# Spreading the start addresses of a block kernel's weight, input and activation buffers modulo 512 bytes

## Chip, cores and metric

The kernel runs on one core of a Trainium2 chip. The metric is device time in microseconds for one execution of the whole kernel; lower is better. All numbers in memory are fp32.

## The reference

With depth 1 the reference is one layer: a gated short convolution, then an expert-choice mixture of experts, over 2048 tokens of width 1024, with 16 experts that take 256 tokens each. Cut to what is computed:

```python
m = silu(c) @ ada_w + ada_b                      # six modulation vectors
hl = modulate(rms_norm(x, norm_g[0]), sh1, sc1)  # 2048 x 1024
gate_b, gate_c, v = split(hl @ w_in, 3)          # weights 1024 x 3072
yl = (gate_b * dwconv(gate_c * v, conv)) @ w_out # weights 1024 x 1024
lat = x + g1 * yl
h2 = modulate(rms_norm(lat, norm_g[1]), sh2, sc2)
aff = softmax(h2 @ router)
g, idx = top_k(aff.T, 256)                       # tokens of each expert
hid = silu(h2[idx] @ w_gate) * (h2[idx] @ w_up)  # per expert, 1024 x 1024 each
out = lat + g2 * scatter_add(idx, (hid @ w_down) * g)
```

## The kernel before

Every large product is made of three products in the type fp32r. Each operand is split into a high part (the value cast to fp32r) and a low part (what is left); high x high, high x low and low x high are added up in PSUM. So a weight slot `ws` holds two halves of 4096 bytes in each partition, and the input tiles hold two halves as well.

**Weights.** All weights pass through one list of pieces of 128 x 1024 numbers. SyncE loads a piece into one of three `raw` buffers (`load_piece`), ScalarE casts it into the first half of a slot (`split_high`, L198), VectorE, in some places GpSimd, subtracts to make the second half (`split_low`, L208). There are eight slots (`n_split`), used in turn.

**Stages.** (1) Input product, `in_mm` (L436, L437, L439): 128 columns of a slot are loaded into the array, and 512 columns of the input tile `hl` are streamed past them; nine matmuls to each of eight contraction steps, 32 such groups. (2) Output product and router, `out_mm` (L641, L642, L644): here a block of `hl` is loaded and 512 columns of a slot are streamed, six matmuls to each contraction step; the router's small products (L708, L709) stand among them. (3) A search for the thresholds of each expert's 256 tokens. (4) The experts: `gate_up` (L1010, L1012, L1014) loads 128 columns of a slot and streams 256 columns of the expert's gathered input `xT`; `down` (L1032 to L1034) loads 128 columns of the activations `hT` and streams 512 columns of a slot. From the third expert on one period is `gate_up` of a half, `down` of half of the expert before, and the same again.

**Order.** Nothing is moved by a scheduler: the program runs as written, and a matmul waits only where its slot, its input or its PSUM bank is not ready. Each matmul has a load of its own, which the array takes while the matmul before it still streams.

**Addresses.** Tiles are placed one behind the other in each partition. In the built program before the change all eight slots start at 384 modulo 512 (they are 8192 bytes apart), all `hl` buffers at 288, and `xs`, both `xT` and all four `hT` at 64. The *distance* of a matmul is here the start of the operand that is being loaded (for the next matmul) minus the start of the one that is streamed, modulo 512. Offsets inside these tiles are multiples of 512, so before the change each product has one distance: 96 in `in_mm`, 416 in `out_mm`, 320 in `gate_up`, 192 in `down`. Where one product follows another, the distance is another for that one matmul: 0 from `down` to `gate_up`, for instance.

The pools are `weights` (`raw` and `ws`), `small`, and `mix` (stages 1 and 2: `hl` and work tiles), whose room is later taken by `moe` (stage 4: `xs`, `xT`, `hT`, `sg`, `ot`). A tile of `moe` waits for the last users of the room that it takes.

Of the kernel before, what the change touches and what calls it, by code (L numbers as in the profile page):

```python
# [7 lines left out]
F32 = mybir.dt.float32  # L8
F32R = mybir.dt.float32r
# [7 lines left out]
P = 128  # L17
# [3 lines left out]
CAP = 256  # L21
KD = D // P
# [18 lines left out]
def block_kernel(ctx: ExitStack, tc, x, c, ada_w, ada_b, norm_g, w_in, conv, w_out, router, wg, wu, wd, out):  # L41
# [3 lines left out]
    wpool = ctx.enter_context(tc.tile_pool(name="weights", bufs=1))  # L45
# [3 lines left out]
    n_raw, n_split = 3, 8  # L49
# [120 lines left out]
    pieces, n_load, n_high, n_done = [], 0, 0, 0  # L170
    ws_of = {}
# [15 lines left out]
    def load_to(i):  # L187
        nonlocal n_load
        while n_load <= min(i, len(pieces) - 1, load_end[0] - 1):
            load_piece(n_load)  # L190
            n_load += 1

    def split_high(i):
        nonlocal n_high
        while n_high <= min(i, len(pieces) - 1):
            load_to(n_high)
            t = wpool.tile([P, 2] + pieces[n_high][3], F32R, name="ws", tag="ws", bufs=n_split)
            nc.scalar.activation(t[:, 0], raws[n_high], AF.Copy)  # L198
            ws_of[n_high] = t
            n_high += 1  # L200

    def split_low(i, eng=None, part=0, n=1):
        nonlocal n_done
        split_high(i)
        t, raw = ws_of[i], raws[i]
        w = pieces[i][3][-1] // n
        s = slice(part * w, (part + 1) * w)
        (eng or nc.vector).tensor_sub(t[:, 1, ..., s], raw[..., s], t[:, 0, ..., s].bitcast(F32))  # L208
        if part == n - 1:
            raws.pop(i)  # L210
            n_done += 1
            load_to(i + n_raw)
# [16 lines left out]
    def split_half(i, g, eng=None):  # L229
        nonlocal n_high, n_done  # L230
        if g == 0:
            ws_of[i] = wpool.tile([P, 2] + pieces[i][3], F32R, name="ws", tag="ws", bufs=n_split)
            n_high += 1
        t, n = ws_of[i], pieces[i][3][0] // 2
        s = slice(g * n, (g + 1) * n)
        nc.scalar.activation(t[:, 0, s], raws[i][:, s], AF.Copy)
        (eng or nc.vector).tensor_sub(t[:, 1, s], raws[i][:, s], t[:, 0, s].bitcast(F32))
        if g:
            raws.pop(i)
            n_done += 1  # L240
            load_to(i + n_raw)
# [106 lines left out]
    with tc.tile_pool(name="mix", bufs=1) as mix:  # L348
# [9 lines left out]

        junk = mix.tile([P, D], BF, name="junk")
        carry = mix.tile([P, KD, 3], F32, name="carry")  # L360
        nc.gpsimd.memset(carry, 0.0)

        hl, xq = {}, {}
# [157 lines left out]
        ada_fix(0, pcol)  # L521
        pair = [new_banks() for _ in range(2)]
        split_half(0, 0)
        split_half(1, 0)
        split_half(2, 0, nc.gpsimd)
        to_hl(0, 0, lambda: ada_cols(1, 0, 4))
        ada_cols(1, 4)
# [411 lines left out]


    moe = ctx.enter_context(tc.tile_pool(name="moe", bufs=1, reuse_waits="tile"))
    out_rows = out.rearrange("b t d -> (b t) d")
    H = QT
    idx_of, gate_of, xT_of, hT_of, ot_of, scat = {}, {}, {}, {}, {}, {}
# [34 lines left out]
    def fetch(e, i, bank=None):  # L979
        g, s = divmod(i, 2)  # L980
        if i == 0:
            xT_of[e] = moe.tile([P, 2, KD, CAP], F32R, name="xT", tag="xT", bufs=2)
        xT, xs = xT_of[e], xs_of[e][s]
        pt = (bank or tp).tile([P, 4, P], F32, name="pt", tag="mm" if bank else "tp")
        for j in range(4):
            nc.tensor.transpose(pt[:, j], xs[:, (4 * g + j) * P:(4 * g + j + 1) * P], identf)  # L986
        d = (slice(None), slice(4 * g, 4 * g + 4), slice(s * P, (s + 1) * P))
        nc.scalar.activation(xT[:, 0][d], pt, AF.Copy)
        nc.vector.tensor_sub(xT[:, 1][d], pt, xT[:, 0][d].bitcast(F32))  # L989

    def gate_up(e, fh, between=lambda k: None):
        xT = xT_of[e]
        if fh == 0:
            hT_of[e] = {}
        ps = [[mm.tile([P, 2, CAP], F32, name="pm", tag="mm") for _ in range(2)] for _ in range(2)]
        for kk in range(KD // 2):
            for j in range(2):
                k = 2 * kk + j
                n = w_moe[0, e, fh, kk] + n_split - 2 + j
                if (e, fh) != (0, 1):  # L1000
                    split_high(n)
                between(k)
                while n_done <= min(n, len(pieces) - 1):
                    split_low(n_done, nc.gpsimd if n_done % 2 and (e, fh) < (1, 1) else None)
                for f in range(4):
                    c0 = slice(f * P, (f + 1) * P)
                    for m in range(2):
                        o = ps[m][f // 2][:, f % 2]
                        w = ws_of[w_moe[m, e, fh, kk]]
                        nc.tensor.matmul(o, w[:, 0, j, c0], xT[:, 0, k], start=(k == 0 and f % 2 == 0), stop=False,  # L1010
                                         skip_group_check=True)
                        nc.tensor.matmul(o, w[:, 0, j, c0], xT[:, 1, k], start=False, stop=False,  # L1012
                                         skip_group_check=True)
                        nc.tensor.matmul(o, w[:, 1, j, c0], xT[:, 0, k], start=False, stop=(k == KD - 1),  # L1014
                                         skip_group_check=True)
        hT = moe.tile([P, 2, 4, CAP], F32R, name="hT", tag="hT", bufs=4)
        hT_of[e][fh] = hT
        for f2 in range(2):
            sg = moe.tile([P, 2, CAP], F32, name="sg", tag="sg", bufs=2)
            nc.scalar.activation(sg, ps[0][f2], AF.Silu)  # L1020
            nc.vector.tensor_mul(sg, sg, ps[1][f2])
            t = slice(2 * f2, 2 * f2 + 2)
            nc.scalar.activation(hT[:, 0, t], sg, AF.Copy)
            nc.vector.tensor_sub(hT[:, 1, t], sg, hT[:, 0, t].bitcast(F32))
# [55 lines left out]
    for i in (0, 2, 1, 3):  # L1080
        fetch(0, i, mm)
    for e in range(E):
        if e == 0:
            gate_up(0, 0, lambda k: (tick(k), pick(1) if k == 7 else None))
            gate_up(0, 1, lambda k: fetch(1, k - 4) if k >= 4 else tick(k) if k > 1 else None)
            continue
        if e == 1:
            gate_up(1, 0, lambda k: tick(k) if k > 1 else None)
            down(0, 0, lambda kk: tick(kk) if kk else None)
            for _ in rounds:  # L1090
                pass
            pick_oh(2)
            gate_up(1, 1, lambda k: pick(2) if k == 2 else None)
        else:
            if e + 1 < E:
                pick_oh(e + 1)
            gate_up(e, 0)
            down(e - 1, 0, (lambda kk: pick(e + 1) if kk == 2 else None) if e + 1 < E else (lambda kk: None))
            gate_up(e, 1)
        down(e - 1, 1, (lambda kk: (fetch(e + 1, kk - 1), fetch(e + 1, kk)) if kk % 2 else None)  # L1100
             if e + 1 < E else (lambda kk: None))
# [24 lines left out]
```

## Time and profile before

| | us |
|---|---|
| median of three runs (lowest, highest) | 1984.61 (1983.23, 1985.26) |
| the profiled execution's own time | 1985.33 |
| its span, from first to last instruction | 1983.5 |
| PE busy | 1901.4 (96%) |
| DVE busy | 1130.6 (57%) |
| ACT busy | 751.2 (38%) |
| POOL busy | 306.9 (15%) |

The profiled execution's time stands 0.7 us above the median. A matmul's busy time in the profile covers its whole passage through the array, and neighbours overlap: a row that says 277 ns for one does not mean that one starts every 277 ns. What a matmul costs is read from the *starts*: the difference of two start times, divided by the number of matmuls between them, here called the pace. [...]

### The profile page before, as it was taken

How to read it: one execution, taken by the hardware profiler on the slowest of the kernel's cores; microseconds unless marked ns; L12 is line 12 of the kernel's file. 1: busy time of each engine (PE TensorE's matmuls, PEld its weight loads, DVE VectorE, ACT ScalarE, POOL GpSimd, SP SyncE). 2: the span in 40 equal slices, each digit the busy share in tenths (PEclk: the TensorE clock that was granted, in tenths of full speed). 3: DMA queues.
4: the chain of work that ended last, by engine and by line, in shares of the span. 5: the costliest groups of instructions: out<-in, count | busy, mean ns of one | idle time of the engine just before them, and what ended most of it. 6: DMA issues, size and time to landing. Idle time of an engine off the chain costs nothing.

```text
span 1983.5 us, 29691 instructions
## 1 busy us (share of the span) xinstructions
PE 1901.4 (96%) x11930; PEld 1669.5 (84%) x11930; DVE 1130.6 (57%) x1656; ACT 751.2 (38%) x1050; POOL 306.9 (15%) x521
## 2 busy tenths in 40 slices
PE   4999999999999999659999999999999999999998
PEld 3787788887788888549999999999999999999996
DVE  7544424344334666776665656656665666566653
ACT  3411126211123333345444544444444444444542
POOL 3310011101011222333211011101110110111001
PEclk8999999999999999869999999999999999999999
DMA  9443241433216443235677676767677766777674
GB/s 283 127 133 127 81 144 53 139 127 123 67 64 213 166 149 132 85 127 165 199 222 211 214 233 200 220 217 235 202 214 233 227 201 214 229 209 218 212 212 116
DMA packets 216573, 344.38 MB, mean 174 GB/s; under 512 B 12092, under 2 KB 94068, under 8 KB 216436
## 3 DMA queue, kind: packets, MB, share of 16 engines
q1 hardware_dynamic: 200468, 284.82, 44.6%
q0 software_dynamic: 15968, 57.68, 11.2%
q8 instruction: 93, 1.52, 0.3%
q14 instruction: 44, 0.36, 0.1%
HBM read 300.51 MB, written 41.94 MB: 173 GB/s over the span
## 4 chain that ended last, share of the span: by engine, by line
PE 92%; DVE 3%; DMA 2%; SPq 1%; issue 1%; ACT 1%; POOL 0%; POOLq 0%; DVEq 0%; ACTq 0%
PE pm L1010 11%; PE pm L1012 11%; PE pm L1014 11%; PE pm L436 9%; PE pm L437 9%; PE pm L439 9%; PE pm L1032 6%; PE pm L1034 6%; PE pm L1033 6%; PE pm L641 3%; PE pm L644 3%; PE pm L642 3%; PE pt L986 1%; SPq L399 1%; DVE hl L312 1%
## 5 line engine op out<-in xcount | busy, mean ns | idle before, releaser
L208 DVE TENSOR_TENSOR ws<-raw,ws 128x1024 fp32r<-128x1024 f32 x415 | 499.0, 1223 | 314.4 <-ACT ws L198 312.5
L198 ACT ACTIVATE ws<-raw 128x1024 fp32r<-128x1024 f32 x437 | 451.0, 1054 | 444.2 <-PE pm L1014 208.0
L1010 PE MATMUL pm<-xT,ws 128*128 128x256 f32 x2048 | 569.6, 278 | 0.0
L1012 PE MATMUL pm<-xT,ws 128*128 128x256 f32 x2048 | 567.7, 277 | 0.1
L1014 PE MATMUL pm<-xT,ws 128*128 128x256 f32 x2048 | 567.4, 277 | 0.0
L1012 PEld LDWEIGHTS pm<-xT,ws 128*128 128x128 f32 x2048 | 386.4, 189 | 1.7 <-DVE xT L989 0.4
L1010 PEld LDWEIGHTS pm<-xT,ws 128*128 128x128 f32 x2048 | 386.2, 189 | 1.2
L1014 PEld LDWEIGHTS pm<-xT,ws 128*128 128x128 f32 x2048 | 386.0, 189 | 0.0
L436 PE MATMUL pm<-hl,ws 128*128 128x512 f32 x768 | 311.2, 405 | 1.0 <-ACT hl L386 1.0
L437 PE MATMUL pm<-hl,ws 128*128 128x512 f32 x768 | 307.0, 400 | 0.0
L439 PE MATMUL pm<-hl,ws 128*128 128x512 f32 x768 | 222.7, 398 | 0.0
L1032 PE MATMUL pm<-ws,hT 128*128 128x512 f32 x512 | 203.8, 398 | 0.0
L1034 PE MATMUL pm<-ws,hT 128*128 128x512 f32 x512 | 201.5, 394 | 0.0
L1033 PE MATMUL pm<-ws,hT 128*128 128x512 f32 x512 | 200.0, 391 | 0.0
L436 PEld LDWEIGHTS pm<-hl,ws 128*128 128x128 f32 x768 | 146.4, 191 | 36.6 <-ACT hl L386 1.4
L437 PEld LDWEIGHTS pm<-hl,ws 128*128 128x128 f32 x768 | 146.4, 191 | 35.1 <-issue 1.0
L439 PEld LDWEIGHTS pm<-hl,ws 128*128 128x128 f32 x768 | 145.8, 190 | 35.8
L1058 POOL DMA_INDIRECT out_dram<-ot,idx x32 | 78.5, 2454 | 591.4 <-DVE ot L1052 587.4
L449 DVE TENSOR_TENSOR u<-cs,pm 128x512 f32<-128x512 f32 x32 | 22.5, 703 | 246.0 <-ACT cs L446 246.0
L446 ACT ACTIVATE cs<-pm 128x512 f32<-128x512 f32 x32 | 19.1, 597 | 346.8 <-issue 272.0
L1034 PEld LDWEIGHTS pm<-ws,hT 128*128 128x128 f32 x512 | 96.2, 188 | 20.7
L1033 PEld LDWEIGHTS pm<-ws,hT 128*128 128x128 f32 x512 | 96.3, 188 | 18.9
(267 smaller groups left out, 2026.8 us busy)
## 6 DMA issues: line engine op xcount, KB each, us to landing
raw<-in_moe_w_gate_dram SPq DMA_DIRECT2D x128, 512.0 KB, 4.4
raw<-in_moe_w_up_dram SPq DMA_DIRECT2D x128, 512.0 KB, 4.3
raw<-in_moe_w_down_dram SPq DMA_DIRECT2D x128, 512.0 KB, 4.6
raw<-in_sc_w_in_dram SPq DMA_DIRECT2D x45, 512.0 KB, 4.6
xt<-in_x_dram SPq DMA_DIRECT2D x32, 512.0 KB, 6.2
aw<-in_ada_w_dram SPq DMA_DIRECT2D x32, 512.0 KB, 6.5
hl<-in_ada_w_dram SPq DMA_DIRECT2D x32, 256.0 KB, 5.4
hl<-vscr SPq DMA_DIRECT2D x16, 512.0 KB, 5.0
```

The lines of the kernel that those rows point to most:

```text
L198: nc.scalar.activation(t[:, 0], raws[n_high], AF.Copy)
L208: (eng or nc.vector).tensor_sub(t[:, 1, ..., s], raw[..., s], t[:, 0, ..., s].bitcast(F32))
L436: nc.tensor.matmul(ps[m], wh, t[:, 0], start=(k == 0), stop=False)
L437: nc.tensor.matmul(ps[m], wl, t[:, 0], start=False, stop=False)
L439: nc.tensor.matmul(ps[m], W(k, m)[0], t[:, 1], start=False, stop=(k == KD - 1))
L1010: nc.tensor.matmul(o, w[:, 0, j, c0], xT[:, 0, k], start=(k == 0 and f % 2 == 0), stop=False, skip_group_check=True)
L1012: nc.tensor.matmul(o, w[:, 0, j, c0], xT[:, 1, k], start=False, stop=False, skip_group_check=True)
L1014: nc.tensor.matmul(o, w[:, 1, j, c0], xT[:, 0, k], start=False, stop=(k == KD - 1), skip_group_check=True)
L1032: nc.tensor.matmul(ps[s], h, w[:, 0, j], start=(k == 0), stop=False)
L1033: nc.tensor.matmul(ps[s], h, w[:, 1, j], start=False, stop=False)
L1034: nc.tensor.matmul(ps[s], l, w[:, 0, j], start=False, stop=(k == KD - 1))
L1058: st = nc.gpsimd.indirect_dma_start(out=out_rows, out_offset=bass.IndirectOffsetOnAxis(ap=idx_of[e][:, s:s + 1], axis=0), in_=ots[s], in_o ...
```

## The change

It moves only the places of tiles. The eight slots get a tag each, and there is a pad of 64 bytes ahead of slots 1 to 7, so that they start at 384, 448, 0, 64, 128, 192, 256 and 320 modulo 512. A pad of 32 bytes in `mix` puts the `hl` buffers at 256. A pad of 64 bytes opens `moe`, one of 64 bytes stands ahead of the second `xT` and one of 128 bytes ahead of each `hT` but the first: `xs` stays at 64, `xT` is at 64 for even experts and at 128 for odd ones, the four `hT` are at 64, 256, 384 and 0.

A distance is then always a multiple of 64. In `in_mm`, `out_mm` and `gate_up` all eight multiples occur equally often, and the distance changes from one slot to the next: in `gate_up` after every third matmul. In `down` it is 192, 256, 448 or 0, seldom 128 or 384.

```diff
--- before.py
+++ after.py
@@ -190,11 +190,17 @@
             load_piece(n_load)
             n_load += 1
 
+    def ws_tile(i):
+
+        if 0 < i < n_split:
+            wpool.tile([P, 16], F32, name=f"wpad{i}")
+        return wpool.tile([P, 2] + pieces[i][3], F32R, name="ws", tag=f"ws{i % n_split}", bufs=1)
+
     def split_high(i):
         nonlocal n_high
         while n_high <= min(i, len(pieces) - 1):
             load_to(n_high)
-            t = wpool.tile([P, 2] + pieces[n_high][3], F32R, name="ws", tag="ws", bufs=n_split)
+            t = ws_tile(n_high)
             nc.scalar.activation(t[:, 0], raws[n_high], AF.Copy)
             ws_of[n_high] = t
             n_high += 1
@@ -229,7 +235,7 @@
     def split_half(i, g, eng=None):
         nonlocal n_high, n_done
         if g == 0:
-            ws_of[i] = wpool.tile([P, 2] + pieces[i][3], F32R, name="ws", tag="ws", bufs=n_split)
+            ws_of[i] = ws_tile(i)
             n_high += 1
         t, n = ws_of[i], pieces[i][3][0] // 2
         s = slice(g * n, (g + 1) * n)
@@ -358,6 +364,7 @@
 
         junk = mix.tile([P, D], BF, name="junk")
         carry = mix.tile([P, KD, 3], F32, name="carry")
+        mix.tile([P, 8], F32, name="mixpad")
         nc.gpsimd.memset(carry, 0.0)
 
         hl, xq = {}, {}
@@ -939,6 +946,7 @@
 
 
     moe = ctx.enter_context(tc.tile_pool(name="moe", bufs=1, reuse_waits="tile"))
+    moe.tile([P, 16], F32, name="moepad")
     out_rows = out.rearrange("b t d -> (b t) d")
     H = QT
     idx_of, gate_of, xT_of, hT_of, ot_of, scat = {}, {}, {}, {}, {}, {}
@@ -979,7 +987,9 @@
     def fetch(e, i, bank=None):
         g, s = divmod(i, 2)
         if i == 0:
-            xT_of[e] = moe.tile([P, 2, KD, CAP], F32R, name="xT", tag="xT", bufs=2)
+            if e == 1:
+                moe.tile([P, 16], F32, name="xpad")
+            xT_of[e] = moe.tile([P, 2, KD, CAP], F32R, name="xT", tag=f"xT{e % 2}", bufs=1)
         xT, xs = xT_of[e], xs_of[e][s]
         pt = (bank or tp).tile([P, 4, P], F32, name="pt", tag="mm" if bank else "tp")
         for j in range(4):
@@ -1013,7 +1023,10 @@
                                          skip_group_check=True)
                         nc.tensor.matmul(o, w[:, 1, j, c0], xT[:, 0, k], start=False, stop=(k == KD - 1),
                                          skip_group_check=True)
-        hT = moe.tile([P, 2, 4, CAP], F32R, name="hT", tag="hT", bufs=4)
+        h_i = (2 * e + fh) % 4
+        if 0 < 2 * e + fh < 4:
+            moe.tile([P, 32], F32, name=f"hpad{h_i}")
+        hT = moe.tile([P, 2, 4, CAP], F32R, name="hT", tag=f"hT{h_i}", bufs=1)
         hT_of[e][fh] = hT
         for f2 in range(2):
             sg = moe.tile([P, 2, CAP], F32, name="sg", tag="sg", bufs=2)
```

No instruction of the computation is added, removed or moved on any engine, and the waits of PE, GpSimd and SyncE are the same. Since `moe` takes other parts of the room of `mix`, some waits for that room stand elsewhere on ScalarE and VectorE. One such place is ScalarE at the second half of the first expert: `sg` is the SwiGLU's product, `hT` its cast, and the queues DMASW1, 3 and 7 are those of stores that GpSimd issued in stages 1 and 2. Before:

```order
L198 ACTIVATE ws<-raw 128x1024 [waits DMAHW4_49,Pool_49]
L1020 ACTIVATE sg<-pm 128x512 [waits PE_49]
L1023 ACTIVATE hT<-sg 128x512 [waits DMASW1_49,DVE_49]
L1020 ACTIVATE sg<-pm 128x512 [waits PE_49]
L1023 ACTIVATE hT<-sg 128x512 [waits DVE_49]
```

After:

```order
L204 ACTIVATE ws<-raw 128x1024 [waits DMAHW4_49,Pool_49]
L1033 ACTIVATE sg<-pm 128x512 [waits PE_49]
L1036 ACTIVATE hT<-sg 128x512 [waits DMASW7_49,DMASW3_49,DVE_49]
L1033 ACTIVATE sg<-pm 128x512 [waits PE_49]
L1036 ACTIVATE hT<-sg 128x512 [waits DVE_49]
```

The order is the same; the first cast of this half waits for other store queues.

## Rows read from the trace of the kernel before

**Rows 1.** The page: busy times, and the chain that ended last by engine.

```profile
PE 1901.4 (96%) x11930; PEld 1669.5 (84%) x11930; DVE 1130.6 (57%) x1656; ACT 751.2 (38%) x1050; POOL 306.9 (15%) x521
PE 92%; DVE 3%; DMA 2%; SPq 1%; issue 1%; ACT 1%; POOL 0%; POOLq 0%; DVEq 0%; ACTq 0%
```

**Rows 2.** Groups by line, engine PE: shapes xcount | busy us, mean ns.

```profile
L1010 PE MATMUL pm<-xT,ws 128*128 128x256 f32 x2048 | 569.6, 278 | 0.0
L436 PE MATMUL pm<-hl,ws 128*128 128x512 f32 x768 | 311.2, 405 | 1.0 <-ACT hl L386 1.0
L1032 PE MATMUL pm<-ws,hT 128*128 128x512 f32 x512 | 203.8, 398 | 0.0
L641 PE MATMUL pm<-ws,hl 128*128 128x512 f32 x256 | 106.2, 415 | 0.0
```

**Rows 3.** Chain in order of time (start us, us, what), input product.

```profile
100.71 0.70 PE pm L439 x3
...
166.07 0.70 PE pm L439 x3
```

**Rows 4.** Timeline of PE (start us, us, what), output product.

```profile
648.62 0.39 PE L641 MATMUL pm<-ws,hl 128*128 128x512 f32 x1
...
651.42 0.39 PE L641 MATMUL pm<-ws,hl 128*128 128x512 f32 x1
```

**Rows 5.** Timeline of PE, `down` and the matmul behind it.

```profile
1304.50 0.39 PE L1033 MATMUL pm<-ws,hT 128*128 128x512 f32 x1
...
1309.54 0.40 PE L1034 MATMUL pm<-ws,hT 128*128 128x512 f32 x1
1309.77 0.28 PE L1010 MATMUL pm<-xT,ws 128*128 128x256 f32 x1
```

**Rows 6.** Timeline of PE, `gate_up`, settled.

```profile
1279.79 0.28 PE L1014 MATMUL pm<-xT,ws 128*128 128x256 f32 x1
...
1283.42 0.28 PE L1012 MATMUL pm<-xT,ws 128*128 128x256 f32 x1
```

**Rows 7.** Timeline of PE, first matmuls of that `gate_up`.

```profile
1276.48 0.28 PE L1010 MATMUL pm<-xT,ws 128*128 128x256 f32 x1
...
1277.18 0.28 PE L1010 MATMUL pm<-xT,ws 128*128 128x256 f32 x1
...
1279.00 0.28 PE L1012 MATMUL pm<-xT,ws 128*128 128x256 f32 x1
```

**Rows 8.** Timeline of PE, `gate_up` of expert 1, second half.

```profile
976.32 0.28 PE L1014 MATMUL pm<-xT,ws 128*128 128x256 f32 x1
...
979.97 0.28 PE L1010 MATMUL pm<-xT,ws 128*128 128x256 f32 x1
```

**Rows 9.** Timeline of PE and its loads (PEld), output product into router.

```profile
643.35 0.19 PEld L642 LDWEIGHTS pm<-ws,hl 128*128 128x128 f32 x1
...
643.82 0.63 PE L644 MATMUL pm<-ws,hl 128*128 128x512 f32 x2
644.05 0.11 PEld L708 LDWEIGHTS plt<-hl,rts 128*32 128x32 f32 x1
644.28 0.22 PE L708 MATMUL plt<-hl,rts 128*32 128x128 f32 x1
```

**Rows 10.** Timeline of PE, input product, early.

```profile
49.16 0.63 PE L436 MATMUL pm<-hl,ws 128*128 128x512 f32 x1
...
50.44 0.63 PE L437 MATMUL pm<-hl,ws 128*128 128x512 f32 x1
```

**Rows 11.** Windows: us, busy (x) of engines, PE clock, DMA share, GB/s.

```profile
50.00:51.00 1.00, 1.00 (x4) 0.79 (x3) 0.97 (x4) 0.88 (x2) 0.04 (x1) 0.50 1.01 401
1130.96:1876.13 745.17, 745.17 (x5630) 698.50 (x5628) 462.21 (x539) 342.08 (x396) 80.49 (x55) 1.00 0.72 218
```

**Rows 12.** Chain in order of time, eight transposes in fp32.

```profile
1883.51 0.87 PE pt L986 x8
```

**Rows 13.** Line L681, GpSimd stores of the second stage.

```profile
L681 POOL DMA_DIRECT2D hscr<-u x15: 620/634/643, 632.5 to 817.6; - x15
DMA to landing us min/median/max: 3.0/3.7/4.6
```

**Rows 14.** Line L1023, the casts into `hT`.

```profile
L1023 ACT ACTIVATE hT<-sg x64: 631/632/634, 904.0 to 1943.4; 128x512 fp32r<-128x512 f32 x64
```

## Prediction, made blind

> **What bounds the kernel.** The page comes first: PE is busy for 96% of the span and holds 92% of the chain that ended last [rows 1]. The change touches no instruction, so it can act only on how fast PE streams, or on an engine that feeds PE. The groups by line give the counts [rows 2]: three lines of 2048 are the 6144 matmuls of `gate_up`, three of 768 the 2304 of `in_mm`, three of 512 the 1536 of `down`, three of 256 the 768 of `out_mm`. Their busy times overlap, so the cost is read as a pace from starts:
>
> - `in_mm`: 65.36 us between two rows of the chain, 31 groups of nine matmuls, so 65.36 / 279 = 234.3 ns [rows 3];
> - `out_mm`: 2.80 us for 12 matmuls, 233.3 ns [rows 4];
> - `down`: 5.04 us for 22 matmuls, 229.1 ns [rows 5];
> - `gate_up`, settled: 3.63 us for 32 matmuls, 113.4 ns [rows 6].
>
> [...] And it differs between products of one shape: `in_mm`, `out_mm` and `down` all stream 512 columns past a loaded block of 128, yet differ by 5 ns. What sets `in_mm` and `out_mm` apart from `down` and `gate_up` is that their distances, 96 and 416, are 32 more than a multiple of 64, while 192 and 320 are multiples of 64.
>
> **The change, part by part.** *Removed and added:* nothing. *Moved waits:* ScalarE's and VectorE's waits for the room of `mix` are for stores; of the last of these, those of `hscr`, the last is issued at 817.6 us and lands within 4.6 us, while the first cast into `hT` starts at 904.0 [rows 13, 14]. Whoever waits for them instead finds them done, some 80 us early: 0 us. *Weights, casts, subtractions, DMAs:* the same sizes and counts, off the path in stage 4 (in the long window DVE is busy for 462 of 745 us, ACT for 342, the DMA share is 0.72 [rows 11]): 0 us, and they have room for a PE that is a few per cent faster.
>
> *`in_mm` and `out_mm`:* their distances become multiples of 64, as those of `down` are now. The trace has no row of these two products at such a distance in a steady run, so I bound it. [...] Worst: the slowest pace that fp32r shows at a multiple of 64 is that of an unsettled `gate_up`, 117.7 ns for 256 columns [rows 8], so 235.4 for 512: 2304 x 1.1 + 768 x 2.1 = 4 us more. I take the row that is nearest in shape, `down` with the same 512 columns and a distance that is a multiple of 64: 234.3 - 229.1 = 5.2 ns for 2304 and 233.3 - 229.1 = 4.2 ns for 768, so 12.0 + 3.2 = 15.2 us.
>
> *`down`:* stays at a multiple of 64, only at several of them. Value taken: 0 us; bounds: 1536 x 13.7 = 21 us less (the floor) and 1536 x 5.2 = 8 us more (the pace of `in_mm`).
>
> *`gate_up`:* the same holds, 0 us taken. [...]
>
> Sum: 1985.3 of the profiled execution - 15.2 = 1970.1 us. The median of the runs stands 0.7 us lower than that execution, which is within what I round: 1970 us.
>
> [...] In the trace, the matmul under which only 32 columns are loaded, for the router, at distance 0, keeps the pace: two matmuls take 643.82 to 644.28, 230 ns each [rows 9], and the one that ends `down`, at distance 0 instead of 192, also takes 230 ns [rows 5]. [...]
>
> **Rivals.**
>
> *1. `gate_up` loses its step (slower).* The same instructions at the same addresses have a second pace: for expert 1 the second half runs at 3.65 us for 31 matmuls, 117.7 ns [rows 8], against 113.4. And each `gate_up` opens at that slower pace: the first six matmuls of one take 0.70 us, 116.7 ns each, before it settles [rows 7]. So loads and streams fall into a rhythm after about six matmuls, if nothing disturbs them. After the change the distance differs every third matmul. If each change of distance starts the settling anew, all 6144 stay at 117.7: 6144 x 4.3 = 26 us more, 2012 us; with the gain in `in_mm` and `out_mm` beside it, 1997. It decides against the change as soon as more than 15.2 / 26 = 58% of these matmuls don't settle. Against it: the jump from distance 192 over 0 to 320, where `down` ends, is repaired within those six matmuls, and a step of 64 may be no disturbance at all.
>
> [...]
>
> *3. Nothing (same).* [...] The rows of the switches speak for it.
>
> **How the numbers follow.** The measurement tells some 0.2%, 4 us, from no change. The forecast, `in_mm` and `out_mm` gain and the rest stays within a few us, has 0.36; rival 2, in whole or half, 0.16; rival 3 0.24; rival 1, enough to outweigh the gain, 0.24. So faster 0.52, same 0.24, slower 0.24. The range goes from 1928 us, just past the half of rival 2 (0.08 lies below), to 2002 us, which holds rival 1 with the gain beside it and most of its single form's partial cases (0.10 lies above). The forecast's own range, with `down` and `gate_up` a little off zero, is 1955 to 1979 us.
>
> **What would show it.** Right: groups of nine `in_mm` matmuls at 2.06 us instead of 2.11, six of `out_mm` at 1.37 to 1.38 instead of 1.40, `down` at 229 ns and settled `gate_up` at 113.4. Rival 1: `gate_up` starts near 117 ns apart beyond its first six matmuls. [...] Rival 3: all four paces as before. Wrong in kind would be a change of DVE or ACT durations, a new wait for a slot, or a stretch of PE at the lower clock.

## The result and the profile after

The change makes the kernel slower: 2003.11 us (four runs, 2002.79 to 2007.04) against 1984.71 before, a ratio of 1.0098 with a 95% interval of 1.0081 to 1.0116. That is 1 us above the forecast range, and 33 us above the forecast.

The page of the changed kernel shows as many matmuls and weight loads as before; PE and its loads (PEld) are busier, the other engines hardly differ [rows 1]:

```profile
span 2001.6 us, 29694 instructions
PE 1921.2 (96%) x11930; PEld 1693.8 (85%) x11930; DVE 1129.5 (56%) x1656; ACT 750.2 (37%) x1050; POOL 308.8 (15%) x521
PE 93%; DVE 4%; issue 1%; DMA 1%; ACT 1%; POOL 1%; SPq 0%; POOLq 0%; DVEq 0%; ACTq 0%
```

In stage 4 PE is busy without a break and at the upper clock, as before (the same stretch as in [rows 11]: window, then PE, PEld, DVE, ACT and POOL busy, clock, DMA share, GB/s). There are simply fewer matmuls in it, 5476 instead of 5630, and with them less work for the other engines:

```profile
1130.96:1876.13 745.17, 745.17 (x5476) 698.68 (x5475) 449.41 (x526) 332.29 (x383) 81.40 (x55) 1.00 0.70 213
```

The four paces, each from two starts. First `gate_up` (now L1020 to L1024), which answers to [rows 6]: 4.97 us for 42 matmuls are 118.3 ns, against 113.4 before. The mean hides a difference: from the third expert on, experts with an even number run at 117.7 ns and those with an odd number at 118.8, though both visit the same distances equally often, only in another order.

```profile
1290.04 0.28 PE L1020 MATMUL pm<-xT,ws 128*128 128x256 f32 x1
...
1295.01 0.28 PE L1020 MATMUL pm<-xT,ws 128*128 128x256 f32 x1
```

`in_mm` (L446), which answers to [rows 3]: 14.61 us for seven groups of nine are 231.9 ns, against 234.3.

```profile
101.88 0.70 PE pm L446 x3
...
116.49 0.70 PE pm L446 x3
```

`out_mm` [rows 4], six matmuls in 1.39 us, 231.7 ns against 233.3; and `down` [rows 5], here 22 matmuls in 5.04 us, 229.1 ns as before, while other stretches of it are slower:

```profile
649.05 0.40 PE L648 MATMUL pm<-ws,hl 128*128 128x512 f32 x1
...
650.44 0.39 PE L648 MATMUL pm<-ws,hl 128*128 128x512 f32 x1
```

```profile
1304.07 0.40 PE L1046 MATMUL pm<-ws,hT 128*128 128x512 f32 x1
...
1309.11 0.40 PE L1047 MATMUL pm<-ws,hT 128*128 128x512 f32 x1
```

Added up over the whole trace, as differences of neighbouring starts (waits included), the span's 18.1 us come out to 0.2 us:

| us | before | after | difference |
|---|---|---|---|
| `gate_up` | 710.6 | 735.4 | +24.8 |
| `in_mm` | 557.7 | 550.7 | -7.0 |
| `out_mm` | 187.4 | 186.3 | -1.1 |
| `down` | 355.7 | 357.3 | +1.6 |
| all else | 160.0 | 160.0 | 0.0 |

So two things that the prediction spoke of happened together: `in_mm` and `out_mm` gain, and `gate_up` loses three times as much as the two gain. From the third expert on `gate_up` loses 25.7 us; in the first two, where waits and small matmuls of other products interrupt it, it loses nothing.

### The profile page after: what moved, and what is told of

The parts are those of the page before. It is cut to its first block, busy times and chain, and to the rows that moved or that the text cites. A ratio compares the mean times of both kernels' runs of the same rounds, so it can differ in the third digit from the quotient of the medians.

```text
span 2001.6 us, 29694 instructions
## 1 busy us (share of the span) xinstructions
PE 1921.2 (96%) x11930; PEld 1693.8 (85%) x11930; DVE 1129.5 (56%) x1656; ACT 750.2 (37%) x1050; POOL 308.8 (15%) x521
## 4 chain that ended last, share of the span: by engine, by line
PE 93%; DVE 4%; issue 1%; DMA 1%; ACT 1%; POOL 1%; SPq 0%; POOLq 0%; DVEq 0%; ACTq 0%
PE pm L1020 12%; PE pm L1022 12%; PE pm L1024 12%; PE pm L443 9%; PE pm L446 9%; PE pm L444 9%; PE pm L1045 6%; PE pm L1047 6%; PE pm L1046 6%; PE pm L648 3%; PE pm L649 3%; PE pm L651 3%; PE pt L996 1%; DVE acc L421 1%; DVE hl L318 1%
## 5 line engine op out<-in xcount | busy, mean ns | idle before, releaser
L1020 PE MATMUL pm<-xT,ws 128*128 128x256 f32 x2048 | 578.4, 282 | 0.0
L1022 PE MATMUL pm<-xT,ws 128*128 128x256 f32 x2048 | 576.4, 281 | 0.1
L1024 PE MATMUL pm<-xT,ws 128*128 128x256 f32 x2048 | 576.3, 281 | 0.0
L1020 PEld LDWEIGHTS pm<-xT,ws 128*128 128x128 f32 x2048 | 388.2, 190 | 1.1
L1024 PEld LDWEIGHTS pm<-xT,ws 128*128 128x128 f32 x2048 | 387.7, 189 | 0.0
L446 PE MATMUL pm<-hl,ws 128*128 128x512 f32 x768 | 220.2, 395 | 0.0
L446 PEld LDWEIGHTS pm<-hl,ws 128*128 128x128 f32 x768 | 145.2, 189 | 33.4
```

The costliest lines, as they stand in the source:

```text
L446: nc.tensor.matmul(ps[m], W(k, m)[0], t[:, 1], start=False, stop=(k == KD - 1))
```

## The experiments

Distances are those of the section on the kernel before. Kernels marked with one run were timed once, beside one or more runs of the kernel before on the same chip.

### Is it the changing, or the place?

Two theories stood against each other: A, a distance that changes every third matmul never lets `gate_up` settle (the first rival); B, some distances are slow in themselves. **e1** takes the changing away: slots all at 384, but each expert's `xT` and `hT` 32 bytes further on.

```diff
+        mix.tile([P, 120], F32, name="mixpad")
...
-            xT_of[e] = moe.tile([P, 2, KD, CAP], F32R, name="xT", tag="xT", bufs=2)
+            room = moe.tile([P, 2 * KD * CAP + 128], F32R, name="xT", tag="xT", bufs=2)
+            o = 8 * e
+            xT_of[e] = room[:, o:o + 2 * KD * CAP].rearrange("p (a k c) -> p a k c", a=2, k=KD)
...
-        hT = moe.tile([P, 2, 4, CAP], F32R, name="hT", tag="hT", bufs=4)
+        room = moe.tile([P, 2 * 4 * CAP + 128], F32R, name="hT", tag="hT", bufs=4)
+        o = 8 * e
+        hT = room[:, o:o + 2 * 4 * CAP].rearrange("p (a k c) -> p a k c", a=2, k=4)
```

> All slots back at 384 modulo 512, so that a distance never changes inside one expert's product. Each expert's xT and hT start 32 bytes further on than the last one's, so the sixteen experts show gate_up at the distances 320, 288, ... in steps of 32, and down at 192, 224, ...; hl is at 256, so in_mm runs at the one distance 128 and out_mm at 384. Theory A (what counts is that the distance changes): every expert's gate_up settles at 113.4 ns after its first matmuls, whatever its distance. Theory B (some distances or places are slow in themselves): the experts whose distance is among those that are slow run their whole gate_up at 117 to 119 ns, the others at 113.4, and the sixteen differ by their distance alone. For in_mm the forecast's step says 229.1 ns at 128; the average pace of the changed kernel says 231.7. Whole kernel: A and 231.7 about 1978 us; B with half the distances slow about 1991.

Measured: 2009.2 us (one run; before beside it 1984.2), longer than either theory's figure. Two stretches of `gate_up` in its timeline: expert 8, at distance 64, takes 1.81 us for 16 matmuls, 113.1 ns; expert 10, at distance 0, takes 1.32 us for 11, 120.0 ns, and its mean over all its matmuls is 120.0 too, although nothing changes.

```profile
1423.76 0.28 PE L1013 MATMUL pm<-xT,ws 128*128 128x256 f32 x1
...
1425.57 0.28 PE L1015 MATMUL pm<-xT,ws 128*128 128x256 f32 x1
```

```profile
1592.54 0.28 PE L1017 MATMUL pm<-xT,ws 128*128 128x256 f32 x1
...
1593.86 0.28 PE L1015 MATMUL pm<-xT,ws 128*128 128x256 f32 x1
```

Theory A as the whole story falls. The sixteen experts give a map, below, and it repeats after 256 bytes: 64 and 320 are fast, 114.0 ns on average, and all others slow, 116.7 to 120.0 (fourteen of sixteen, not half, hence the longer time). And `in_mm`, here at the one distance 128, runs at 232.7 ns, not at the 229.1 that the prediction took for any multiple of 64.

**e4** moves the other operand: the weights inside the slot, 32 bytes further for each channel tile of `in_mm` and for each expert. (One work buffer fewer makes the room.)

```diff
+        t = wpool.tile([P, 2 * D + 64], F32R, name="ws", tag="ws", bufs=n_split)
+        o = 8 * (i // 3 % 8) if i < 48 else 40 if i < 56 else shift_of[i]
+        t = t[:, o:o + 2 * D]
...
+                shift_of[len(pieces)] = 8 * (e % 8)
```

> Slots lie at 384 and 128 in turn, and inside a slot the weights start 32 bytes further for each of the eight channel tiles of a half in in_mm, so that in_mm runs 144 matmuls or more at each of the eight distances 96, 128, ... 320 (modulo 256: all eight steps of 32); out_mm runs at distance 0 modulo 256; the experts' weights start 32 bytes further from one expert to the next (eight steps), so gate_up runs at 64, 96, ... and down at 192, 160, ... modulo 256. (One work buffer fewer in stages 1 and 2 pays for the room, which may add stalls there; the paces tell.) Theory B, pace is a fixed function of the distance modulo 256 whichever operand is moved: gate_up repeats the run before, 113.4 at 64, 120 at 0, 117.8 at 192, 116.7 at 224, and down 227.8 at 0, 229 at 192. in_mm differs between its eight distances by several ns, 234.3 again at 96 and 232.7 at 128. Theory D (in_mm's loss has nothing to do with the distance): all eight at 232 to 234 in no order.

Measured: 2008.37 us (one run; before 1980.97). Theory D falls, B holds. Mean differences of neighbouring starts inside each product, in ns, by distance modulo 256, waits left out:

| | 0 | 32 | 64 | 96 | 128 | 160 | 192 | 224 |
|---|---|---|---|---|---|---|---|---|
| `gate_up`, e1 (xT moved) | 120.0 | 118.3 | 114.0 | 118.7 | 118.7 | 120.0 | 117.8 | 116.7 |
| `gate_up`, e4 (weights moved) | 120.0 | 118.3 | 114.9 | 118.3 | 118.7 | 120.0 | 117.8 | 116.7 |
| `down`, e1 (hT moved) | 227.8 | 232.9 | 233.2 | 234.2 | 233.1 | 233.4 | 229.1 | 233.0 |
| `down`, e4 (weights moved) | 227.9 | 232.9 | 233.3 | 233.9 | 232.3 | 233.7 | 230.5 | 233.3 |
| `in_mm`, e4 (weights moved) | 226.9 | 233.3 | 233.4 | 234.2 | 232.3 | 233.3 | 229.1 | 233.3 |

Whichever operand is moved, the same distance has nearly the same pace, and the two products that stream 512 columns have nearly the same rows. Only the mean at 64 is no single pace: in e4 the first half of expert 8 ran at 117.8 ns and the second at 113.4, at the same distance (more on this below). Among these steps the kernel before had `gate_up` at 320, its best place, `down` at 192, its second best, and `in_mm` at 96, its worst.

### The period, and whether a change costs anything

**e5** has e4's slot tile without its shifts: neighbouring slots lie 256 bytes apart modulo 512.

```diff
+        t = wpool.tile([P, 2 * D + 64], F32R, name="ws", tag="ws", bufs=n_split)
+        o = 0
+        t = t[:, o:o + 2 * D]
```

> As in the kernel before, but neighbouring slots lie 256 bytes apart modulo 512: the distance changes after every third matmul of gate_up, between 320 and 64. Theory B with the period 256: gate_up settles at 113.4 ns as before the change, in_mm at 234.3, out_mm at 233.3, down at 229; the kernel takes what it took before, plus what one work buffer fewer costs in stages 1 and 2. Theory A (a changing distance never settles) or a period of 512: gate_up near 117.8 ns, 26 us more in stage 4.

Measured: 1984.65 us (one run; before 1980.97). Its `gate_up` alternates between 320 and 64 every third matmul and holds 113.2 ns, 28 matmuls in 3.17 us; `in_mm` 234.3, `out_mm` 233.2, `down` 229.0. The period of 256 holds: a change by 256 costs nothing. Modulo 256 that is no change at all, so this run does not tell what other changes do; e2 and e3 below do.

```profile
1276.75 0.28 PE L1021 MATMUL pm<-xT,ws 128*128 128x256 f32 x1
...
1279.92 0.28 PE L1023 MATMUL pm<-xT,ws 128*128 128x256 f32 x1
```

### Which pads did it

**e3** has the slot pads alone.

```diff
+        if i < n_split and ws_pads[i]:
+            wpool.tile([P, ws_pads[i]], F32, name=f"wpad{i}")
+        t = wpool.tile([P, 2] + pieces[i][3], F32R, name="ws", tag=f"ws{i % n_split}", bufs=1)
```

> The slot pads alone: slots 64 bytes apart modulo 512 as in the change, but xT, hT at 64 and hl at 288 as before it. Theories A and B: gate_up at 118 ns as in the changed kernel, since only the slots matter there. Theory C (the moved xT and hT slow it): gate_up at 113.4 ns. For in_mm: if its gain comes from the half line of 32 bytes (hl at 256), it is back at 234 ns and the kernel takes about 2010 us; if it comes from the mixture of distances, it is at 232 ns and the kernel takes about 2003 us.

Measured: 2004.97 us (one run), `gate_up` 117.7, `in_mm` 232.0 with `hl` at 288. Theory C falls: the slots slow `gate_up`. And `in_mm` gains with the 32 bytes still there, so the gain is the mixture of distances. The map does not add up here: modulo 256 `in_mm` visits 32, 96, 160 and 224, of which none runs below 233.3 ns in e4, and yet the mixture runs at 232.0.

**e2** has e3's code and the slots in pairs, so that the distance changes only every 48th matmul of `gate_up`.

```diff
+    ws_pads, ws_tail = [0, 0, 16, 0, 16, 0, 16, 0], 80
```

> Slots in pairs: 384, 384, 448, 448, 0, 0, 64, 64 modulo 512; xT and hT at 64 and hl at 288 as before the change. gate_up takes its gate weights from the even slot and its up weights from the odd slot of a pair, so its distance changes only every 48th matmul instead of every third. Theory A: about six matmuls of 48 are unsettled, mean pace 113.4 + 4.3 x 6 / 48 = 113.9 ns, whole kernel within 5 us of 1988. Theory B: the distances 320, 384, 448 and 0 are all among those at which the changed kernel runs at 117.5 to 119, so gate_up stays at 117 to 119 ns, whole kernel about 2010 us.

Measured: 2011.02 us (one run), `gate_up` 118.5. By distance: 119.8 at 0, 118.7 at 384, 117.7 at 448. But 320 runs at 117.7 as well, for all 48 matmuls, and there the map says 113.4. So distance 64 modulo 256 has two paces, as [rows 7] and [rows 8] had shown.

Together e2 and e3 tell what changes cost `gate_up`, which visits 0, 64, 128 and 192 modulo 256 equally often in both. With the slower pace at 64, the map's mean is (120.0 + 117.8 + 118.7 + 117.8) / 4 = 118.6. With a change every 48th matmul it runs at 118.5, so the map adds up; with a change every third matmul it runs at 117.7, a little faster. Frequent changes therefore do not cost `gate_up` anything here, but they do move its pace by about 1 ns, and no run shows how.

**e8** moves `xT` alone, to 384.

```diff
+            if e == 0:
+                moe.tile([P, 80], F32, name="xpad")
...
+        if (e, fh) == (0, 0):
+            moe.tile([P, 48], F32, name="hpad")
```

> The kernel before with one thing moved: xT at 384, so that gate_up alone runs at the one distance 0, never changing; hT back at 64, hl at 288. Theory B: gate_up at 120.0 ns, 6144 x 6.3 = 39 us more, about 2023 us. Theory A (only changing distances cost): 1985 us.

Measured: 2020.27 us (four runs, 2019.60 to 2021.24), ratio 1.0183, interval 1.0168 to 1.0199. `gate_up` takes 4.20 us for 35 matmuls, 120.0 ns; `in_mm` takes 67.47 us for 32 groups of nine, 234.3 ns, as before. One constant, unlucky distance costs more than the whole change did.

```profile
1299.73 0.28 PE L1016 MATMUL pm<-xT,ws 128*128 128x256 f32 x1
...
1303.93 0.28 PE L1014 MATMUL pm<-xT,ws 128*128 128x256 f32 x1
```

```profile
97.62 0.71 PE pm L439 x3
...
165.09 0.70 PE pm L439 x3
```

**e7** maps in steps of 8 bytes, with the shifts of e4 for `in_mm` and of e1 for the experts.

```diff
+        o = 2 * (i // 3 % 8) if i < 48 else 0
...
+            o = 2 * e
...
+        o = 2 * e
```

> The map in steps of 8 bytes: in_mm from distance -32 to 24 by channel tile, down from 192 to 312 by expert, gate_up from 128 down to 8 by expert. If the loss is set by which 64 bytes the two operands are in, the pace is flat inside 64 bytes and jumps at its ends; if by 32 bytes or 16, it has steps of that size. [...] No claim on the whole time.

Measured (one run, 2009.88 us): the best places are narrow. `in_mm` 226.8 at 0, but 230.7 at 8 and 233.3 at 16 and 248; `gate_up` at 64 117.8 in one half of its expert and 113.5 in the other, but 120.1 at 56 and 120.0 at 72. Neither of the expected steps, and nothing below the best of the coarse map. But the coarse map misses places: at 240, between its steps, `in_mm` runs at 228.3, better than at 192.

### A kernel from the map, and what it ran into

**e6** is the kernel before with two pads, for `in_mm`, `out_mm` and `down` at 0 modulo 256.

```diff
+        mix.tile([P, 24], F32, name="mixpad")
...
+        if (e, fh) == (0, 0):
+            moe.tile([P, 16], F32, name="hpad")
```

> The kernel before with two pads only: 96 bytes that put hl at 384, so that in_mm and out_mm run at distance 0, and 64 bytes that put hT at 128, so that down runs at 256, which is 0 modulo 256. gate_up stays at 320. Theory B: in_mm 226.9 ns instead of 234.3 (2304 x 7.4 = 17 us less), out_mm 229.1 instead of 233.3 (3 us less), down 227.8 instead of 229.0 (2 us less), gate_up unchanged: about 1963 us, ratio 0.989. If the paces per distance held only for the kernels in which slots or inputs move about, nothing changes: 1985 us.

Measured: 1985.35 us (eleven runs), ratio 1.0007, interval 0.9998 to 1.0016: no change. Three terms came as expected (`in_mm` 227.1, `out_mm` 228.8, `down` 227.5 ns). But `gate_up`, with not one of its own addresses changed, ran at 117.8 from the third expert on and took 731.4 us instead of 710.6, which is nearly all that the three had gained. Two kernels tell why. **e9** has the pad in `mix` alone:

```diff
+        mix.tile([P, 24], F32, name="mixpad")
```

> The kernel before with one pad of 96 bytes in mix, so that hl lies at 384: in_mm and out_mm at distance 0, everything of the experts as before. Theory E (gate_up at 64 modulo 256 has a fast and a slow rhythm, and which of them it falls into is decided by the product in front of it; down at 192 leads into the fast one): gate_up settles at 113.4 again, down at 229, in_mm 227.0, out_mm 228.8, so 2304 x 7.2 + 768 x 4.5 = 20 us less than before, about 1964 us. Theory F (gate_up turned slow because of hl, or because everything behind starts earlier): gate_up at 117.6, about 1988 us.

**e10** has the pad ahead of `hT` alone:

```diff
+        if (e, fh) == (0, 0):
+            moe.tile([P, 16], F32, name="hpad")
```

> The kernel before with one pad of 64 bytes ahead of hT, so that down runs at 256 (0 modulo 256) and nothing else moves. Theory E: down 227.5 ns instead of 229.0, 2 us less, and gate_up, though its own addresses are unchanged, stays at 117.6 ns, 6144 x 3.9 = 24 us more: about 2006 us. Theory F: gate_up at 113.4, about 1982 us.

Measured: e9 1963.17 us (four runs, 1961.73 to 1964.70; before 1984.32), ratio 0.9892, interval 0.9876 to 0.9909; e10 2006.19 us (one run). In e9 `in_mm` takes 57.12 us for 28 groups of nine, 226.7 ns:

```profile
108.26 0.68 PE pm L440 x3
...
165.38 0.68 PE pm L440 x3
```

A `gate_up` of e9, behind `down` at 192: the first six matmuls take 0.70 us, the next 28 take 3.17 us, 113.2 ns.

```profile
1289.13 0.28 PE L1011 MATMUL pm<-xT,ws 128*128 128x256 f32 x1
...
1289.83 0.28 PE L1011 MATMUL pm<-xT,ws 128*128 128x256 f32 x1
...
1293.00 0.28 PE L1013 MATMUL pm<-xT,ws 128*128 128x256 f32 x1
```

One of e10, behind `down` at 256: 4.12 us for 35 matmuls, 117.7 ns, and it never settles.

```profile
1292.82 0.28 PE L1014 MATMUL pm<-xT,ws 128*128 128x256 f32 x1
...
1296.94 0.28 PE L1012 MATMUL pm<-xT,ws 128*128 128x256 f32 x1
```

Per expert, from eleven periods between equal transposes in the chain: e9 (1856.48 - 1110.32) / 11 = 67.83 us, e10 (1896.90 - 1134.21) / 11 = 69.33 us.

```profile
1110.32 0.87 PE pt L987 x8
...
1856.48 0.87 PE pt L987 x8
```

```profile
1134.21 0.87 PE pt L986 x8
...
1896.90 0.87 PE pt L986 x8
```

Theory F falls: moving `down` alone changes the pace of `gate_up` behind it. (The pad also moves what is placed behind `hT`, such as `sg` and `ot`, which PE doesn't read.) e4 and e7 show the same inside one kernel. In e4 expert 8's first half, behind a `down` at distance 0 modulo 256, ran at 117.8 ns, and its second, behind one at 224, at 113.4; in e7 it was 117.8 behind 240 and 113.5 behind 248. From the third expert on, in all eight traces with halves of `gate_up` that run at 64 throughout, the first matmul of such a half starts 226 or 227 ns after the last one of `down` where it turns out slow, and 229 to 236 ns after it where it turns out fast. That fits a rhythm set at the start; how it is set isn't shown.

What stands in front need not be a long product. In the kernel before itself, the half of expert 1 of [rows 8] ran at 1.47 us for 13 matmuls, 113.1 ns, until sixteen small matmuls of another step (L962) and a short wait came in the middle of it; behind them it ran at 117.8 to its end, for 142 matmuls, though nothing disturbed it.

```profile
972.79 0.28 PE L1010 MATMUL pm<-xT,ws 128*128 128x256 f32 x1
...
974.26 0.28 PE L1012 MATMUL pm<-xT,ws 128*128 128x256 f32 x1
974.38 0.28 PE L1014 MATMUL pm<-xT,ws 128*128 128x256 f32 x1
974.50 0.46 PE L962 MATMUL pi<-ax,oh 128*128 128x10 bf16 x12
975.18 0.26 PE L962 MATMUL pi<-ax,oh 128*128 128x10 bf16 x4 [0.23 <-DVE oh L954]
```

And in e10, in the first half of expert 1, one small matmul of the search (L865) turned the slower pace into the faster: 2.00 us for 17 matmuls in front of it, 117.6 ns, and 2.27 us for 20 behind it, 113.5 ns. The next one, with a wait beside it, turned it back.

```profile
936.40 0.28 PE L1014 MATMUL pm<-xT,ws 128*128 128x256 f32 x1
...
938.40 0.28 PE L1012 MATMUL pm<-xT,ws 128*128 128x256 f32 x1
938.64 0.17 PE L865 MATMUL pc<-cnt,same 128*128 128x4 f32 x1
939.10 0.28 PE L1010 MATMUL pm<-xT,ws 128*128 128x256 f32 x1
...
941.37 0.28 PE L1014 MATMUL pm<-xT,ws 128*128 128x256 f32 x1
```

In the five kernels with all of `gate_up` at 64 (before, e5, e6, e9, e10), every uninterrupted stretch of 20 or more of its matmuls keeps one of the two paces after its first eight or so. e9 is faster than both kernels of this study, with one pad of 96 bytes.

## Why the prediction was wrong

**The bound was right.** PE's pace was what moved: the clock in stage 4 stayed at 1.00, VectorE and ScalarE were busy for 1129.5 and 750.2 us against 1130.6 and 751.2, and all that PE did outside the four products took 160.0 us both times, so the moved waits of ScalarE and VectorE show no cost.

**The step that failed** is the one on `gate_up`: "the same holds, 0 us taken". It rested on the reading that every multiple of 64 is as good as 320. Measured were +24.8 us. e1 and e4 show in its place that 320 was the best of all distances in steps of 32, 113.4 ns where the others take 116.7 to 120.0, and that 64 modulo 256, which the change visits in one slot of four, then runs at its slower pace, 117.8 in the changed kernel. e8 shows the price of leaving 320 by itself: `gate_up` alone at 0 costs 36 us.

**The term for `in_mm` and `out_mm`** had the right sign and was too large: 15.2 us forecast, 8.1 measured. Its reason was wrong, so the sign was luck. Being a multiple of 64 is not what helps (e4: 233.4 at 64, 233.3 at 32); `down` was fast because it stood at 192 (229.1 in e1). The mixture of all multiples of 64 averages 231.7, and e3's mixture of distances that all lie 32 off such a multiple does as well, 232.0; a constant 0 gives 227. `down` lost 1.6 us where 0 was taken, inside its bounds.

**The rows that misled** were those of the single switches at distance 0 [rows 5, 9]: one matmul at another distance keeps the pace of its neighbours, and I read that as a pace that doesn't depend on the distance. Both rows are of matmuls with 512 columns, and for these 0 is the best of all distances (227 ns), so they could not have shown a loss. e8 holds the same distance 0 for a whole stage of matmuls with 256 columns and costs 36 us. Of what PE reads, e8 moves only the streamed operand, and PE's pace goes from 113.4 to 120.0 ns; by e1 and e4 it is the place of the one operand against the other that counts.

**The first rival** named the place, the sign and nearly the price (26 us, 1997 with the gain; 24.8 and 2003 measured, since the gain was half as large). Its mechanism was half right. That `gate_up` has two paces and needs a favourable start, which it took from [rows 7, 8], is what e2, e6 and e10 show. That it settles after about six matmuls if nothing disturbs it is not so: the half of [rows 8] had 142 undisturbed matmuls and did not. And it is not the changes of distance that cost, since e2, which changes sixteen times less often, is no faster than the changed kernel (118.5 and 118.2 ns, on average from the third expert on). The mean of the map at 0, 64, 128 and 192, (120.0 + 113.4 + 118.7 + 117.8) / 4 = 117.5, is 4.1 ns above 113.4 and explains most of the 4.8 that were lost in these experts; the fast pace at 64, which was never reached, makes (117.8 - 113.4) / 4 = 1.1 more. The sum is 0.4 too large, and by the map the experts with even and odd numbers should not differ (117.7 and 118.8): that part of the mixture stays open.

The second rival (all four products gain) was wrong: `gate_up`, which stood at its best place, lost 24.8 us. The floor in the bound for `down` (21 us less), on which the half of rival 2 and with it the range's lower end of 1928 us rest as well, is shown by no run: the best paces measured are 226.7 ns for 512 columns (e9) and some 113 ns for 256 (113.2 in e5 and e9), and `down` lost 1.6 us. The third (nothing) falls with e8 and e9, where addresses alone move the time by 36 us up and 21 us down.

## What to carry to other kernels

Where back-to-back fp32r matmuls of one shape run at different paces, as here at 229.1 and 234.3 ns, compute the distance between the loaded and the streamed operand modulo 256, the period found here, and measure the pace over a long constant run at each step, for one product at a time, in steps of 8 bytes rather than 32; then give each product a fixed good distance rather than a spread of them. Sum the pace times the count over all products first: a spread takes from the one that happens to stand well. And check the paces of the products behind the one that was moved: here that cost nearly all the gain of three products (e6).

## What the hardware showed beyond expectation

The pace of these products depends on the distance of their two operands with a period of 256 bytes (e1; in e5 `gate_up` holds 113.2 ns at 320 and 64 in turn), and the best place is less than 8 bytes wide on either side (e7): 226.8 ns at 0, 230.7 at 8 and 233.3 at 248 for 512 columns; for 256 columns 113.5 at 64 in the faster half, and 120 at 56 and 72. The same instructions at the same addresses have two stable paces, 113.4 and 117.8 ns, and what stands in front decides which, for all 192 matmuls of a half if nothing interrupts them (e6, e10); even one small matmul in between can turn the one into the other (e10). Why 64 is best for 256 columns and 0 for 512, what repeats after 256 bytes, and why a mixture of distances does not run at the map's mean, no run here tells. Nor was it tried whether a few other matmuls between `down` and `gate_up` would keep e6's three gains without the loss.
